# One core, one decoder layer: the high parts of the weights moved by 128 bytes in SBUF

## The chip, the cores and the metric

The kernel runs on one core of one Trainium2 chip. The metric is the time of one execution in device microseconds (us); lower is better. Times before: 1966.2 us, the median of three runs (1963.88 to 1972.04).

## The reference

One layer on 256 tokens of width 2048, all in float32: a feed-forward block, a token mixer (eight attention heads with a forget gate, four mLSTM heads) and a second feed-forward block, each with a modulated layer norm ahead and a residual layer norm behind. The weights are far larger than the activations: the two feed-forward blocks alone multiply 256 rows with 2048x11264 and 5632x2048 matrices.

```python
def _swiglu(h, w_in, w_out):
    gate, up = jnp.split(h @ w_in, 2, axis=-1)
    return (jax.nn.silu(gate) * up) @ w_out
...
    h = _swiglu(_modulate(x, sh1, sc1), ffn1_w_in, ffn1_w_out)
    x = _layernorm(ALPHA * x + 0.5 * (1 + g1) * h, ln1_g, ln1_b)
    h = _token_mixer(_modulate(x, sh2, sc2), w_in, ...)
    x = _layernorm(ALPHA * x + (1 + g2) * h, ln2_g, ln2_b)
    h = _swiglu(_modulate(x, sh3, sc3), ffn2_w_in, ffn2_w_out)
    x = _layernorm(ALPHA * x + 0.5 * (1 + g3) * h, ln3_g, ln3_b)
```

## The kernel before

**Three products for one.** Each float32 operand is split in two parts of the type that TensorE multiplies fast (`F32R`): `hi` is the value rounded to that type (a cast on ScalarE, L142), `lo` is what is left (a subtraction on VectorE, L143). `mm3` (L372 to L375) then forms one product as hi·hi, hi·lo and lo·hi, three matmuls into one accumulator. In the profile's names, `s<-xhi_f,hi_s` streams `xhi_f` through the array (the moving operand) past `hi_s`, which has been loaded into it before (the stationary operand); the row PEld LDWEIGHTS with the same names is that load.

**Two forms of product.** In form A (`cols_form_a`, L378) the weights are stationary and the activations stream, 256 columns a matmul: `s`, `gu_f`, `fh`, `fs` (input halves of the feed-forward blocks) and `pr_m`, `pr_f` (queries and keys). In form B (`out_proj`, `cols_form_b`, `cols_1024`) the rows of activations are stationary and the weights stream, up to 512 columns a matmul: `o_f` and `o_mx` (the three output projections), `mo`, `ge`, `gf`, `b_fv`, `b_mv`. In `out_proj` the stationary rows are `hh` and `hl` (feed-forward) or `yhi`, `ylo`, `yh`, `yl` (mixer).

**Where the weights go.** `load_w` (L361) reads a block of 1 MB into a buffer `raw` (three of them) and splits it into four pairs `hi`, `lo`; each of the tags `hi` and `lo` has six buffers of 4096 bytes in each partition. The pool `wp` (L52 to L61) lays out these buffers in the order in which it meets them first: the three `raw`, a filler `gap_hi`, the six `hi`, four `sums` (40 bytes each, at every 64th byte, 256 together), four `nm` (128 bytes together), the six `lo`. The functions that ask for a tile of these tags later get one of those places. All buffers of a tag stand 4096 bytes apart, and slices of them begin at multiples of 512 bytes, so that a tag has one place modulo 512 bytes. That remainder, read from the addresses in the built program, is called the place here:

| tiles | place before |
|---|---|
| `raw` (three buffers) | 96, 224, 352 |
| `hi` | 288 |
| `lo` | 160 |
| `hh`, `hl`, `yhi`, `ylo` (rows of the output projections) | 160 |
| `h` (the first pair of row tiles of each feed-forward block's output projection, made ahead) | 448 |
| `yh`, `yl` (rows of the mixer's mLSTM half) | 128 to 392, several |
| `xhi_f`, `xlo_f`, `xhi_mx`, `xlo_mx` (activations of the other products) | 480 |
| `ahi`, `alo` (parts of the modulation's sums) and, stationary beside them, `trir` | 160, 160 and 128 |

**Order.** The order of the matmuls is that of the program; a scheduling layer places the instructions of the other engines. SyncE issues the weights' DMAs, one block ahead of a free `raw` buffer. The modulation matrix (`w_ada`) is read and summed on VectorE beside the products, piece by piece, from `pump`.

Of the kernel before, what the change touches and what calls it, by code (L numbers as in the profile page):

```python
# [34 lines left out]
def layer_kernel(  # L35
# [11 lines left out]
    wp = ctx.enter_context(tc.tile_pool(name="wp", bufs=1))  # L47


    def gap(pool, nbytes, name):  # L50
        pool.tile([P, nbytes // 4], F32, tag=name, name=name)
# [1 line left out]


    wp.tile([P, 4, 520], F32, tag="raw", bufs=3, name="raw_place")
    gap(wp, 320, "gap_hi")
    wp.tile([P, 1024], F32R, tag="hi", bufs=6, name="hi_place")
    wp.tile([P, 10], F32, tag="sums", bufs=4, name="sums_place")
    wp.tile([P, 2, 3], F32, tag="nm", bufs=4, name="nm_place")
    wp.tile([P, 1024], F32R, tag="lo", bufs=6, name="lo_place")  # L60
# [1277 lines left out]
```

## Time and profile before

| | us |
|---|---|
| median of three runs | 1966.2 |
| the profiled execution | 1965.57 |
| its span, first to last instruction | 1963.8 |
| mean granted TensorE clock | 0.993 |
| first feed-forward block, input half | 33 to 541 |
| its output projection | 541 to 786 |
| mixer with its output projection | 786 to 1212 |
| second feed-forward block, input half | 1212 to 1714 |
| its output projection | 1714 to 1951 |

The profile is of one execution. Its span and what lies around it (1.8 us) make that execution's own time, which is 0.6 us under the median. A TensorE row's duration runs from the start of streaming to the modelled end of its results, and the next matmul starts long before that end; the time that a matmul takes from the path is therefore the distance from its start to the next one's start, called the spacing here. The timeline view has the starts, to 0.01 us.

### The profile page before, as it was taken

Reading aid. Unit: us, or ns where it says so; the run is one execution under the profiler, and the core shown is the slowest. Engines: PE = TensorE matmul, PEld = TensorE weight load, DVE = VectorE, ACT = ScalarE, POOL = GpSimd, SP = SyncE. Lnnn points to the kernel's source line nnn. Section 1 sums busy time; section 2 is a strip of 40 time slices with the busy share of each in tenths; the row PEclk is TensorE's granted clock in tenths of the full one; section 3 lists DMA queues with packets and bytes.
Section 4 is the critical chain, followed back from the end, with each engine's and each line's share of the span. In section 5 each row is a group of like instructions: output and inputs, shape, how many; then the busy total and the mean of one; then the engine's idle time right before and its main releaser. Section 6 shows DMA issues by size and latency. Waiting matters only on the chain.

```text
span 1963.8 us, 32259 instructions
## 1 busy us (share of the span) xinstructions
PE 1896.5 (97%) x13057; PEld 1727.6 (88%) x13057; DVE 1495.8 (76%) x1878; ACT 961.1 (49%) x1396; POOL 6.3 (0%) x17
## 2 busy tenths in 40 slices
PE   3999999999999999899999998999999999999997
PEld 3999999999988888588999786899999999988885
DVE  7788889777788897678888688777766655555776
ACT  3644354443454554745755544555444444444553
POOL 0000000000000000000000000000000000000000
PEclk9999999999999999999999999999999999999999
DMA  9998978899898786489888784888777765655552
GB/s 331 342 315 278 314 253 289 290 305 326 281 343 303 268 303 208 140 292 319 270 300 278 273 285 151 285 292 274 241 248 249 261 216 190 236 193 193 193 193 86
DMA packets 301820, 510.89 MB, mean 260 GB/s; under 512 B 10818, under 2 KB 158690, under 8 KB 300648
## 3 DMA queue, kind: packets, MB, share of 16 engines
q1 hardware_dynamic: 300808, 505.70, 76.2%
q0 software_dynamic: 864, 3.15, 0.5%
q8 instruction: 102, 1.67, 0.4%
q14 instruction: 46, 0.38, 0.0%
HBM read 506.71 MB, written 2.10 MB: 259 GB/s over the span
## 4 chain that ended last, share of the span: by engine, by line
PE 83%; DVE 8%; DMA 5%; ACT 2%; issue 2%; SPq 0%; DVEq 0%; ACTq 0%
PE gu_f L374 8%; PE gu_f L375 8%; PE gu_f L373 8%; PE o_f L373 8%; PE o_f L375 8%; PE o_f L374 8%; PE s L373 3%; PE s L375 3%; PE s L374 3%; DMA raw_s<-in_ffn_w_in_dram 2%; DVE lo_s L143 2%; PE fs L375 1%; PE fs L374 1%; PE fs L373 1%; PE o_mx L373 1%
## 5 line engine op out<-in xcount | busy, mean ns | idle before, releaser
L157 DVE SCALAR_TENSOR_TENSOR acc<-ar,csil,acc 128x1024 f32<-128x1024 f32 x242 | 307.8, 1272 | 74.6 <-DMA ar<-in_w_ada_dram 72.9
L373 PE MATMUL s<-xhi_f,hi_s 128*128 128x256 f32 x768 | 215.0, 280 | 3.0 <-ACT hi_s L142 3.0
L375 PE MATMUL s<-xhi_f,lo_s 128*128 128x256 f32 x768 | 214.4, 280 | 1.9 <-DVE lo_s L143 1.9
L374 PE MATMUL s<-xlo_f,hi_s 128*128 128x256 f32 x768 | 214.2, 279 | 0.0
L375 PE MATMUL gu_f<-xhi_f,lo_f2i 128*128 128x256 f32 x768 | 212.0, 276 | 0.0
L373 PE MATMUL gu_f<-xhi_f,hi_f2i 128*128 128x256 f32 x768 | 212.0, 276 | 0.0
L374 PE MATMUL gu_f<-xlo_f,hi_f2i 128*128 128x256 f32 x768 | 212.0, 276 | 0.0
L143 DVE TENSOR_TENSOR lo_f2i<-raw_f2i,hi_f2i 128x1024 fp32r<-128x1024 f32 x96 | 117.6, 1225 | 91.4 <-ACT hi_f2i L142 91.4
L373 PE MATMUL gu_f<-xhi_f,hi_f1i 128*128 128x256 f32 x640 | 176.8, 276 | 0.0
L375 PE MATMUL gu_f<-xhi_f,lo_f1i 128*128 128x256 f32 x640 | 176.7, 276 | 0.0
L374 PE MATMUL gu_f<-xlo_f,hi_f1i 128*128 128x256 f32 x640 | 176.7, 276 | 0.0
L142 ACT CAST hi_f2i<-raw_f2i 128x1024 fp32r<-128x1024 f32 x96 | 100.8, 1050 | 135.4 <-PE gu_f L374 124.6
L373 PEld LDWEIGHTS s<-xhi_f,hi_s 128*128 128x128 f32 x768 | 146.2, 190 | 3.5 <-ACT hi_s L142 3.4
L142 ACT CAST hi_s<-raw_s 128x1024 fp32r<-128x1024 f32 x96 | 96.6, 1049 | 107.0 <-DMA raw_s<-in_ffn_w_in_dram 85.9
L375 PEld LDWEIGHTS s<-xhi_f,lo_s 128*128 128x128 f32 x768 | 145.9, 190 | 2.9 <-DVE lo_s L143 2.8
L374 PEld LDWEIGHTS s<-xlo_f,hi_s 128*128 128x128 f32 x768 | 146.4, 191 | 0.0
L374 PEld LDWEIGHTS gu_f<-xlo_f,hi_f2i 128*128 128x128 f32 x768 | 144.2, 188 | 0.2
L373 PEld LDWEIGHTS gu_f<-xhi_f,hi_f2i 128*128 128x128 f32 x768 | 144.2, 188 | 0.2
L375 PEld LDWEIGHTS gu_f<-xhi_f,lo_f2i 128*128 128x128 f32 x768 | 144.2, 188 | 0.0
L142 ACT CAST hh<-hT 128x512 fp32r<-128x512 f32 x130 | 80.0, 622 | 127.9 <-PE o_f L374 126.6
L143 DVE TENSOR_TENSOR lo_f2o<-raw_f2o,hi_f2o 128x1024 fp32r<-128x1024 f32 x88 | 107.7, 1224 | 44.9 <-ACT hi_f2o L142 44.8
L143 DVE TENSOR_TENSOR lo_s<-raw_s,hi_s 128x1024 fp32r<-128x1024 f32 x96 | 114.5, 1221 | 30.6 <-ACT hi_s L142 30.6
(452 smaller groups left out, 5385.2 us busy)
## 6 DMA issues: line engine op xcount, KB each, us to landing
ar<-in_w_ada_dram SPq DMA_DIRECT2D x288, 512.0 KB, 5.4
raw_s<-in_ffn_w_in_dram SPq DMA_DIRECT2D x48, 1024.0 KB, 6.1
raw_f2i<-in_ffn_w_in_dram SPq DMA_DIRECT2D x48, 1024.0 KB, 5.2
raw_f1o<-in_ffn_w_out_dram SPq DMA_DIRECT2D x44, 1024.0 KB, 7.4
raw_f2o<-in_ffn_w_out_dram SPq DMA_DIRECT2D x44, 1024.0 KB, 5.1
raw_f1i<-in_ffn_w_in_dram SPq DMA_DIRECT2D x40, 1024.0 KB, 7.7
raw_mxo<-in_w_out_dram SPq DMA_DIRECT2D x16, 1024.0 KB, 6.1
raw_fh<-in_ffn_w_in_dram SPq DMA_DIRECT2D x16, 1024.0 KB, 7.3
```

Of the source, the lines that this page charges most:

```text
L142: S.copy(hi, src)
L143: return V.tensor_tensor(out=lo, in0=src, in1=hi.bitcast(F32), op=ALU.subtract)
L157: V.scalar_tensor_tensor(out=acc, in0=raw, scalar=csil[:, k:k + 1], in1=acc, op0=ALU.mult, op1=ALU.add)
L373: PE.matmul(o, ah, bh, start=start, stop=False)
L374: PE.matmul(o, ah, bl, start=False, stop=False)
L375: PE.matmul(o, al, bh, start=False, stop=stop)
```

## The change

The filler ahead of the `hi` buffers shrinks from 320 to 192 bytes, and a new filler of 128 bytes behind them keeps everything that follows where it was. The `hi` buffers move down by 128 bytes, from place 288 to place 160. No other tile moves, and the instructions of all engines, their order, their waits and the DMAs are the same, apart from the addresses of `hi`.

```diff
     wp.tile([P, 4, 520], F32, tag="raw", bufs=3, name="raw_place")
-    gap(wp, 320, "gap_hi")
+    gap(wp, 192, "gap_hi")
     wp.tile([P, 1024], F32R, tag="hi", bufs=6, name="hi_place")
+    gap(wp, 128, "gap_lo")
     wp.tile([P, 10], F32, tag="sums", bufs=4, name="sums_place")
     wp.tile([P, 2, 3], F32, tag="nm", bufs=4, name="nm_place")
     wp.tile([P, 1024], F32R, tag="lo", bufs=6, name="lo_place")
```

## The prediction

> **What bounds the kernel now.** First the page: its span, the busy shares and the chain that ended last.
>
> ```profile
> span 1963.8 us, 32259 instructions
> PE 1896.5 (97%) x13057; PEld 1727.6 (88%) x13057; DVE 1495.8 (76%) x1878; ACT 961.1 (49%) x1396; POOL 6.3 (0%) x17
> PE 83%; DVE 8%; DMA 5%; ACT 2%; issue 2%; SPq 0%; DVEq 0%; ACTq 0%
> ```
>
> TensorE sets the end: 83% of the chain is matmuls. Then the windows, to see where nothing but TensorE counts (columns: length, busy time and instructions of each engine, granted clock, DMA share and GB/s).
>
> ```profile
> core 0: us, PE busy (x) PEld busy (x) DVE busy (x) ACT busy (x) POOL busy (x), PEclk, DMA share, GB/s
> 340.00:540.00 200.00, 200.00 (x1753) 199.48 (x1752) 152.53 (x154) 85.96 (x99) 0.00 (x0) 1.00 0.92 301
> 720.00:780.00 60.00, 60.00 (x264) 49.09 (x263) 50.71 (x61) 30.19 (x39) 0.00 (x0) 1.00 0.72 244
> 1880.00:1940.00 60.00, 60.00 (x264) 49.17 (x263) 43.50 (x48) 32.34 (x42) 0.00 (x0) 1.00 0.44 149
> ```
>
> TensorE is busy throughout, at full clock. In the output projections 264 matmuls touch 60 us in both blocks, though VectorE and the DMAs are much less busy in the second: there the matmuls' own spacing is the limit. So the question is whether the spacing depends on where the operands stand. The timeline gives it (starts in the first column):
>
> ```profile
> 399.81 0.28 PE L375 MATMUL gu_f<-xhi_f,lo_f1i 128*128 128x256 f32 x1
> ...
> 400.49 0.28 PE L375 MATMUL gu_f<-xhi_f,lo_f1i 128*128 128x256 f32 x1
> 541.27 0.40 PE L373 MATMUL o_f<-hi_f1o,h 128*128 128x512 f32 x1
> ...
> 546.63 0.39 PE L375 MATMUL o_f<-hi_f1o,h 128*128 128x512 f32 x1
> 886.35 0.28 PE L373 MATMUL b_mv<-hi_mv,xhi_mx 128*128 128x256 f32 x1
> ...
> 886.70 0.28 PE L373 MATMUL b_mv<-hi_mv,xhi_mx 128*128 128x264 f32 x1
> 1900.11 0.39 PE L373 MATMUL o_f<-hi_f2o,hh 128*128 128x512 f32 x1
> ...
> 1908.81 0.39 PE L375 MATMUL o_f<-hi_f2o,hl 128*128 128x512 f32 x1
> ```
>
> Form A: 0.68 us for 6 steps, 113 ns for 256 columns. Form B in the second projection: 8.70 us for 38 steps, 229 ns for 512 columns. The same form with the rows `h` at place 448 instead of 160: 5.36 us for 23 steps, 233 ns. And 256 columns in form B: 0.35 us for 3 steps, 117 ns. The place is one thing in which the second and third differ, so it can be worth 4 ns a matmul.
>
> **Which pairs of places meet.** A stationary operand is loaded one matmul ahead (first and last start below: 546.6 against 546.9), so while one matmul streams, the next one's rows are loaded. The tile view has minimum, median and maximum durations:
>
> ```profile
> L373 PEld LDWEIGHTS o_f<-hi_f1o,hh x344: 187/188/188, 546.6 to 785.2; 128*128 128x128 f32 x172
> L373 PE MATMUL o_f<-hi_f1o,hh x344: 390/393/393, 546.9 to 785.4; 128*128 128x512 f32 x172
> L374 PE MATMUL o_f<-lo_f1o,hh x344: 388/388/397, 547.1 to 785.6; 128*128 128x512 f32 x172
> L375 PE MATMUL o_f<-hi_f1o,hl x344: 388/391/396, 547.3 to 785.9; 128*128 128x512 f32 x172
> L373 PE MATMUL o_f<-hi_f1o,h x8: 394/396/397, 541.3 to 546.2; 128*128 128x512 f32 x8
> L374 PE MATMUL o_f<-lo_f1o,h x8: 388/395/397, 541.5 to 546.4; 128*128 128x512 f32 x8
> L375 PE MATMUL o_f<-hi_f1o,h x8: 392/397/397, 541.7 to 546.6; 128*128 128x512 f32 x8
> ```
>
> In a trio of `o_f`, L373 streams `hi` (288) while rows at 160 are loaded, L374 streams `lo` (160) while rows at 160 are loaded, L375 streams `hi` (288) over rows at 160: distances of 128, 0 and 128 bytes, durations of 393, 388 and 391. After the change all three distances are 0, and the streamed place no longer changes from one matmul to the next. No row of before has both; the L374 row has the distance alone.
>
> **The change, part by part.**
>
> *Form B with rows at 160.* These are the rows `hh`, `hl`, `yhi` and `ylo`: 344 matmuls on each of three lines in each block and 64 on each of three lines of `o_mx`, which is 2 x 344 + 64 = 752 trios.
>
> ```profile
> L373 PE MATMUL o_mx<-hi_mxo,yhi 128*128 128x512 f32 x64 | 26.3, 411 | 0.0
> L373 PE MATMUL o_f<-hi_f2o,hh 128*128 128x512 f32 x344 | 135.2, 393 | 0.0
> ```
>
> Differences of durations stand here for differences of spacing, since the end is modelled from the start. Lower bound: both `hi` matmuls fall to L374's 388, (393 - 388) + (391 - 388) = 8 ns a trio, 752 x 8 ns = 6.0 us gained. Upper bound: all go to the spacing of the `h` rows, 233 against 229, so 3 x 4.1 ns x 752 = 9.2 us lost. Between them: the `hi` matmuls are nearest to their own rows and to the matched one, but L374's 388 stands between two matmuls of another place, and part of it may be a start that swings late on L373 (393) and is made good on L374. Two matmuls in a row that stream from one place (160) do exist, over another stationary place (128):
>
> ```profile
> L170 PE MATMUL bc<-alo,trir x28: 390/393/503, 359.1 to 1649.0; 128*128 128x512 f32 x28
> ```
>
> The second of such a pair takes 393, no less than the alternating ones. So I leave the two `hi` matmuls at their mean of 392 and let L374 lose half of its advantage over them, 390 instead of 388: +2 ns a trio, 752 x 2 ns = +1.5 us. TensorE has no cover there, so this goes straight to the end.
>
> *Form B with rows at 480 and the mixer's `yh`, `yl`.* Here `lo` is already at the place that `hi` will have.
>
> ```profile
> L373 PE MATMUL gf<-hi_gu,xhi_f x32: 391/392/481, 1335.9 to 1357.4; 128*128 128x512 f32 x32
> L374 PE MATMUL gf<-lo_gu,xhi_f x32: 390/392/393, 1336.2 to 1357.6; 128*128 128x512 f32 x32
> L375 PE MATMUL gf<-hi_gu,xlo_f x32: 388/391/397, 1336.4 to 1357.8; 128*128 128x512 f32 x32
> L374 PE MATMUL o_mx<-lo_mxo,yh x64: 388/393/402, 1123.9 to 1202.8; 128*128 128x512 f32 x64
> ```
>
> 392, 392, 391: against 480 the two places cost the same, so nothing. The 192 matmuls of `yh`, `yl` meet many distances already and stay near 393: nothing; at 4 ns each way they are worth 0.8 us, which both ends of the range take in.
>
> *Form A, some 9200 matmuls* (counted in the program, on each of three lines: 768 of `s`, 640 and 768 of `gu_f`, 256 each of `fh` and `fs`, 12 x 32 of `pr_m` and `pr_f`). The streamed place stays 480; two of three loads move from 288 to 160, where the third, `lo`, already is.
>
> ```profile
> L373 PE MATMUL gu_f<-xhi_f,hi_f2i x768: 276/276/279, 1446.0 to 1708.8; 128*128 128x256 f32 x192
> L374 PE MATMUL gu_f<-xlo_f,hi_f2i x768: 276/276/280, 1446.1 to 1708.9; 128*128 128x256 f32 x192
> L375 PE MATMUL gu_f<-xhi_f,lo_f2i x768: 276/276/285, 1446.3 to 1709.0; 128*128 128x256 f32 x192
> ```
>
> `lo` is loaded while L374 streams, `hi` while the other two do, and all three take 276. So nothing; the rival below has the price if that is wrong.
>
> *ScalarE's cast and VectorE's subtraction.* The cast writes `hi`, the subtraction reads it and writes `lo`, from now on at the same place.
>
> ```profile
> L142 ACT CAST hi_gu<-raw_gu x20: 612/620/674, 1234.1 to 1342.2; 128x512 fp32r<-128x512 f32 x20
> L142 ACT CAST hh<-hT x130: 612/622/639, 542.6 to 1934.4; 128x512 fp32r<-128x512 f32 x130
> L143 DVE TENSOR_TENSOR lo_gu<-raw_gu,hi_gu x20: 681/684/693, 1234.8 to 1345.0; 128x512 fp32r<-128x512 f32 x20
> L143 DVE TENSOR_TENSOR hl<-hT,hh x130: 673/688/693, 545.2 to 1935.1; 128x512 fp32r<-128x512 f32 x130
> ```
>
> At equal width, writing to 288 or 160 takes 620 and 622 ns, and subtracting with unequal or equal places (`hl` from `hh`, both 160) 684 and 688. That is at most 4 ns in 512 columns, 8 in 1024, hidden under the matmuls. Were all of VectorE's 8% of the chain (157 us) longer by 4/684, it would be 0.9 us. I take nothing.
>
> The sum: 1965.57 + 1.5 = 1967.1 us for an execution like the profiled one, which was 0.6 us under the median of the runs; on the median, **1967.7 us**.
>
> **The rivals.**
>
> *The matched place is the good one.* Streaming and loading at one place run at the L374 pace. For it: 388 is the lowest median of the 512-column rows shown, and the unmatched `h` rows the highest. Against it: the `bc` rows. Time: 1966.2 - 6.0 = 1960.2. If the constant streamed place helps on top of that, it could pass 0.5%, 9.8 us, which is about what runs of this kernel can tell from no change; that takes 13 ns a trio.
>
> *The matched place is the bad one* (slower). Streaming and loading start together and meet on the same place in every matmul, where now two of three are 128 bytes apart; L374's short row would then be the swing of its start alone. Place: the output projections. Price: the spacing of the `h` rows, 9.2 us, and 4.1 ns also on the 192 matmuls of `yh`, `yl` and the 432 of 512 columns with rows at 480 (120 of `mo`, 96 of `gf`, 24 of `ge`, 192 of `b_fv` and `b_mv`), 2.6 us: 1978.0. It decides from 4.3 ns a matmul on (9.8 us over 2256). Against it: L374 is at distance 0 now and is not slow.
>
> *Form A loses its floor.* The 113 ns hold with loads from 288, 288 and 160 in turn; 256 columns in form B take 117 with the same pair of places the other way round, so 113 is not given. If three loads from 160 cost that, 9200 x 3.4 ns = 31 us: 1997. Against it: three equal rows of 276.
>
> *The place does nothing* and the `h` rows are slow for another reason (they are the first of the projection): 1966.2. The Trainium skill says so for a part (TensorE: Matmul & The Clock Gate, "Step-by-step: what each phase is for"): TensorE has two read ports into SBUF, and loading the next weights takes no read bandwidth from the running matmul. By that rule no distance matters and the change is worth nothing; the `h` rows, 233 ns against 229, speak against it, though not alone. The same page's "Back-to-back issue gap" puts 512 columns at about 216 ns; the rows here are 13 ns above, and it does not say what they wait for.
>
> **How the numbers follow.** Forecast (spacing within some 3 ns a trio of now) 0.52; matched good 0.18; matched bad 0.18; form A 0.08; no effect of the place 0.04. The range leaves out form A and the far end beyond the `h` rows: from 1960.2 down by 3 for the spread of the runs to 1957, from 1978.0 up by 3 to 1981. Faster by over 0.5%: 0.11, all from the good match with a gain beyond L374's and a little spread. Slower by over 0.5%: form A's 0.08, two thirds of the bad match, 0.12, and 0.01 of spread: 0.21. The rest, 0.68, within.
>
> **What would show it.** In the profile after, the three lines of `o_f` should have one duration instead of three: near 391 if I am right, 388 or less if the match is good, 395 or more if it is bad. A window of 60 us in the second projection should count 264 matmuls again (267 or more: good; 260 or less: bad). The rows of `gu_f` should stay at 276 and their spacing at 113; anything else there is the costly rival. `gf` and `b_mv` should not move, nor the 1220 ns of VectorE's subtractions. I am wrong if the output projections' stages change by more than 3 us each, or any other by more than 1 us.

## The result and the profile after

| | before | after |
|---|---|---|
| median of four runs each, us | 1968.11 (1963.88 to 1972.04) | 1988.57 (1984.12 to 1991.18) |
| the profiled execution, us | 1965.57 | 1989.95 |
| its span, us | 1963.8 | 1988.2 |

The change makes the kernel slower: ratio 1.0099, 95% interval 1.0078 to 1.0120. Ratios here and below are of fast executions alone, and one of the profiles used, pair_160_32's (2017.19 us at a granted clock of 0.989), is of a slow one. The page of the kernel after, its span, busy times and the shares of the chain:

```profile
span 1988.2 us, 32259 instructions
PE 1923.7 (97%) x13057; PEld 1759.5 (88%) x13057; DVE 1496.9 (75%) x1878; ACT 961.6 (48%) x1396; POOL 6.3 (0%) x17
PE 87%; DVE 6%; DMA 4%; ACT 2%; issue 1%; SPq 0%; DVEq 0%; ACTq 0%
```

The number of instructions is the same, and VectorE and ScalarE work as long as before. TensorE is busy 27.2 us longer with the same 13057 matmuls (1923.7 - 1896.5), and the time in which it is idle (span less busy) falls by 2.8 us. So the whole loss is in matmuls that follow each other more slowly. The tile view says which (minimum, median and maximum duration in ns, first and last start in us):

```profile
L374 PE MATMUL gu_f<-xhi_f,hi_f2i x768: 276/279/283, 1465.3 to 1735.4; 128*128 128x256 f32 x192
L375 PE MATMUL gu_f<-xlo_f,hi_f2i x768: 276/279/284, 1465.5 to 1735.5; 128*128 128x256 f32 x192
L376 PE MATMUL gu_f<-xhi_f,lo_f2i x768: 276/280/285, 1465.6 to 1735.7; 128*128 128x256 f32 x192
L374 PE MATMUL o_f<-hi_f1o,hh x344: 387/389/398, 560.2 to 796.5; 128*128 128x512 f32 x172
L375 PE MATMUL o_f<-lo_f1o,hh x344: 387/389/395, 560.4 to 796.7; 128*128 128x512 f32 x172
L376 PE MATMUL o_f<-hi_f1o,hl x344: 388/389/397, 560.6 to 796.9; 128*128 128x512 f32 x172
```

Form A has left its 276: `gu_f` of the second block now runs from 1465.3 to 1735.7, 270.4 us where it was 263.0 (1446.0 to 1709.0). Form B in the output projections has become shorter: the three durations 393, 388 and 391 are one, 389, and the first projection takes 236.7 us from its first `hh` to its last `hl`, where it was 239.0. From the first and last starts of such rows, in both kernels:

| stretch, us | before | after | difference |
|---|---|---|---|
| `s` and `gu_f`, first block | 37.8 to 541.2 | 37.7 to 554.4 | +13.3 |
| `o_f`, `hh` and `hl`, first block | 546.9 to 785.9 | 560.2 to 796.9 | -2.3 |
| from there to the first `fh` (mixer, boundary, `ge`) | 785.9 to 1242.4 | 796.9 to 1255.2 | +1.8 |
| `fh` | 1242.4 to 1335.0 | 1255.2 to 1350.6 | +2.8 |
| `gf`, to the first `fs` | 1335.0 to 1358.1 | 1350.6 to 1374.0 | +0.3 |
| `fs` and `gu_f`, second block | 1358.1 to 1709.0 | 1374.0 to 1735.7 | +10.8 |
| from there to the last `o_f` | 1709.0 to 1950.7 | 1735.7 to 1975.1 | -2.3 |

With what lies between the rows they make the span's 24.4. Summed over starts: 9110 spacings of form A without a wait grow from a mean of 113.52 to 117.00 ns (+31.7 us), and 2110 of `o_f` shrink from 229.07 to 226.94 (-4.5 us); together that is the 27.2 us of busy time.

The mean of 117.0 is not one pace but two. Windows of 40 us of after in form A and one of 60 us in the second projection (TensorE's columns come first; the counts include the two or three matmuls that only reach into a window):

```profile
400.00:440.00 40.00, 40.00 (x342) 40.00 (x342) 29.86 (x29) 16.21 (x18) 0.00 (x0) 1.00 0.97 320
465.00:505.00 40.00, 40.00 (x356) 40.00 (x355) 31.31 (x31) 15.82 (x19) 0.00 (x0) 1.00 0.97 325
1560.00:1600.00 40.00, 40.00 (x342) 40.00 (x341) 23.07 (x22) 15.49 (x17) 0.00 (x0) 1.00 0.74 252
1880.00:1940.00 60.00, 60.00 (x267) 49.69 (x266) 45.57 (x51) 34.57 (x45) 0.00 (x0) 1.00 0.57 193
```

342 or 356 of the same matmuls fit into 40 us: 117.7 or 113 ns each. The first two windows, one of each pace, have the same clock (1.00) and the same DMA share (0.97), and nearly as much work on VectorE and ScalarE beside them; the third is slow at a DMA share of 0.74. In the kernel before, the first two of these windows hold 353 and 355. Where the pace changes, the timeline of after shows it (starts in the first column):

```profile
458.82 0.28 PE L375 MATMUL gu_f<-xlo_f,hi_f1i 128*128 128x256 f32 x1
458.94 0.28 PE L376 MATMUL gu_f<-xhi_f,lo_f1i 128*128 128x256 f32 x1
459.05 0.28 PE L374 MATMUL gu_f<-xhi_f,hi_f1i 128*128 128x256 f32 x1
459.17 0.28 PE L375 MATMUL gu_f<-xlo_f,hi_f1i 128*128 128x256 f32 x1
459.29 0.28 PE L376 MATMUL gu_f<-xhi_f,lo_f1i 128*128 128x256 f32 x1
459.41 0.39 PE L171 MATMUL bc<-ahi,trir 128*128 128x512 f32 x1
459.63 0.39 PE L171 MATMUL bc<-alo,trir 128*128 128x512 f32 x1
459.87 0.28 PE L374 MATMUL gu_f<-xhi_f,hi_f1i 128*128 128x256 f32 x1
459.98 0.28 PE L375 MATMUL gu_f<-xlo_f,hi_f1i 128*128 128x256 f32 x1
...
461.11 0.28 PE L376 MATMUL gu_f<-xhi_f,lo_f1i 128*128 128x256 f32 x1
461.23 0.28 PE L374 MATMUL gu_f<-xhi_f,hi_f1i 128*128 128x256 f32 x1
```

Four steps take 0.47 us ahead of the two `bc` matmuls (458.82 to 459.29) and twelve take 1.36 us behind them (459.87 to 461.23): 117.5 and 113 ns. TensorE does nothing else between. At 519.7 us two more `bc` matmuls turn the pace back. In groups of six matmuls of form A with no wait in them, 1211 of 1478 are slow in after (a mean spacing above 115.5 ns); in before it is 33 of 1479, all within a dozen matmuls behind an interruption. So before, form A falls back to 113 ns each time; after, it keeps whichever pace an interruption leaves it in.

### The profile page after: what moved, and what is told of

Same layout as the page of the kernel before. It is cut to its first block, busy times and chain, and to the rows that moved or that the text cites. A ratio compares the mean times of both kernels' runs of the same rounds, so it can differ in the third digit from the quotient of the medians.

```text
span 1988.2 us, 32259 instructions
## 1 busy us (share of the span) xinstructions
PE 1923.7 (97%) x13057; PEld 1759.5 (88%) x13057; DVE 1496.9 (75%) x1878; ACT 961.6 (48%) x1396; POOL 6.3 (0%) x17
## 4 chain that ended last, share of the span: by engine, by line
PE 87%; DVE 6%; DMA 4%; ACT 2%; issue 1%; SPq 0%; DVEq 0%; ACTq 0%
PE gu_f L376 8%; PE gu_f L374 8%; PE gu_f L375 8%; PE o_f L374 8%; PE o_f L375 8%; PE o_f L376 8%; PE s L376 3%; PE s L374 3%; PE s L375 3%; DMA ar<-in_w_ada_dram 2%; PE pr_f L374 2%; PE fs L374 2%; PE pr_f L376 2%; PE fs L376 2%; PE pr_f L375 2%; PE fs L375 2%
## 5 line engine op out<-in xcount | busy, mean ns | idle before, releaser
L374 PE MATMUL s<-xhi_f,hi_s 128*128 128x256 f32 x768 | 217.0, 283 | 4.8 <-ACT hi_s L143 3.0
L374 PE MATMUL gu_f<-xhi_f,hi_f2i 128*128 128x256 f32 x768 | 213.8, 278 | 0.0
L144 DVE TENSOR_TENSOR lo_f2i<-raw_f2i,hi_f2i 128x1024 fp32r<-128x1024 f32 x96 | 117.5, 1224 | 98.2 <-ACT hi_f2i L143 98.1
L374 PE MATMUL gu_f<-xhi_f,hi_f1i 128*128 128x256 f32 x640 | 178.3, 279 | 0.1
L374 PEld LDWEIGHTS s<-xhi_f,hi_s 128*128 128x128 f32 x768 | 145.9, 190 | 5.6 <-ACT hi_s L143 3.3
L374 PEld LDWEIGHTS gu_f<-xhi_f,hi_f2i 128*128 128x128 f32 x768 | 143.9, 187 | 0.2
L144 DVE TENSOR_TENSOR lo_f2o<-raw_f2o,hi_f2o 128x1024 fp32r<-128x1024 f32 x88 | 107.7, 1224 | 44.3 <-ACT hi_f2o L143 44.2
```

Source lines behind the costliest of these rows:

```text
L144: return V.tensor_tensor(out=lo, in0=src, in1=hi.bitcast(F32), op=ALU.subtract)
L374: PE.matmul(o, ah, bh, start=start, stop=False)
```

## The experiments

Places are given modulo 512 bytes in the text and the diffs, and modulo 256 in the tables, since the runs show that only that counts. "Distance" is the streamed place less the place of the operand loaded meanwhile, modulo 256. In form A the high part is loaded while the first and third line of `mm3` stream, the low part while the second does; in before the distances are 192, 64, 192, in after 64, 64, 64.

**Which part is it: both at 288, exchanged, both at 480, x split.** Each kernel moves places and nothing else; the instructions and their order are those of before. (Beside the parts of the weights, small tiles such as `nm` and `sums` move in some of these kernels and in those of the next two sections, and the layer norms' `n`, `sq` and `xf` in those that move x. No product of form A or B reads them.) The first three edits are against the kernel before, the last against the kernel after:

```diff
 # both_288: hi and lo at 288
-    gap(wp, 320, "gap_hi")
+    wp.tile([P, 2, 3], F32, tag="nm", bufs=4, name="nm_place")
+    gap(wp, 192, "gap_1")
     wp.tile([P, 1024], F32R, tag="hi", bufs=6, name="hi_place")
+    wp.tile([P, 1024], F32R, tag="lo", bufs=6, name="lo_place")
     wp.tile([P, 10], F32, tag="sums", bufs=4, name="sums_place")
-    wp.tile([P, 2, 3], F32, tag="nm", bufs=4, name="nm_place")
-    wp.tile([P, 1024], F32R, tag="lo", bufs=6, name="lo_place")
+    gap(wp, 128, "gap_5")
 # swapped ("exchanged" in the text): hi at 160, lo at 288
-    gap(wp, 320, "gap_hi")
+    wp.tile([P, 2, 3], F32, tag="nm", bufs=4, name="nm_place")
+    gap(wp, 64, "gap_1")
     wp.tile([P, 1024], F32R, tag="hi", bufs=6, name="hi_place")
+    gap(wp, 128, "gap_3")
+    wp.tile([P, 1024], F32R, tag="lo", bufs=6, name="lo_place")
     wp.tile([P, 10], F32, tag="sums", bufs=4, name="sums_place")
-    wp.tile([P, 2, 3], F32, tag="nm", bufs=4, name="nm_place")
-    wp.tile([P, 1024], F32R, tag="lo", bufs=6, name="lo_place")
+    gap(wp, 128, "gap_6")
 # both_480: hi and lo at 480, as x
-    gap(wp, 320, "gap_hi")
     wp.tile([P, 1024], F32R, tag="hi", bufs=6, name="hi_place")
+    wp.tile([P, 1024], F32R, tag="lo", bufs=6, name="lo_place")
     wp.tile([P, 10], F32, tag="sums", bufs=4, name="sums_place")
     wp.tile([P, 2, 3], F32, tag="nm", bufs=4, name="nm_place")
-    wp.tile([P, 1024], F32R, tag="lo", bufs=6, name="lo_place")
+    gap(wp, 320, "gap_4")
 # x_split: as after, xhi of the feed-forward blocks at 352, xlo at 480
-        return (xp.tile([P, KD, T], F32R, name=f"xhi_{tag}"), xp.tile([P, KD, T], F32R, name=f"xlo_{tag}"))
+        xhi = xp.tile([P, KD, T], F32R, name=f"xhi_{tag}")
+        if tag != "mx":
+            gap(xp, 128, f"gap_{tag}")
+        return xhi, xp.tile([P, KD, T], F32R, name=f"xlo_{tag}")
```

> hi and lo both at place 288, nothing else moved. Theory 1 (variety: form A falls back to its 113 ns only where the loads come from two places in turn): all loads come from one place, so the 256-column matmuls stand at 117 to 118 ns for most of their time as in the changed kernel, near 1990 us. Theory 2 (the place itself: loads from 160 are the slow ones over streams at 480, loads from 288 are good): 113 ns throughout, near 1968 us. In form B with rows at 160 both give a distance of 128 for all three, about 229 ns.

> hi at 160 and lo at 288, nothing else moved. Theory 1: two places in turn again, 113 ns in form A, and the output projections between 227 and 231 ns: within 6 us of the kernel before, near 1968 us. Theory 2: two of three loads still come from 160, 116 to 118 ns, near 1985 us.

> hi and lo both at place 480, the same as the streamed activations of form A. Theory 1: one place, so 117 to 118 ns for most of form A, 1985 to 1995 us. Theory 2 says nothing certain of this place; 113 ns here would speak against theory 1. Form B with rows at 160 has a distance of 320 for all three.

> The changed kernel (hi and lo at 160) with xhi of the two feed-forward blocks moved to 352 and xlo left at 480, so that the streamed place alternates in form A and the loads' does not. Theory 1 in its wide form (any alternation of the distance brings the 113 ns back): 113 ns in the feed-forward blocks, the output projections keep the 227 ns of the changed kernel, so 3 to 6 us under the kernel before, near 1964 us. Theory 1 in its narrow form (the loads' places must alternate) and theory 2: 116 to 118 ns, near 1985 us.

All four are slow: ratios to the kernel before 1.0133 (1.0109 to 1.0156), 1.0081 (1.0056 to 1.0105), 1.0268 (1.0250 to 1.0285) and 1.0108 (1.0093 to 1.0123). So neither of the first two theories holds: by the first, exchanged was to be fast, by the second, both_288. x_split refutes the first in its wide form too. The tile view of both_480:

```profile
L373 PE MATMUL gu_f<-xhi_f,hi_f2i x768: 277/283/283, 1481.6 to 1759.5; 128*128 128x256 f32 x192
L373 PE MATMUL o_f<-hi_f1o,hh x344: 396/397/398, 564.8 to 807.7; 128*128 128x512 f32 x172
L373 PE MATMUL gf<-hi_gu,xhi_f x32: 387/389/482, 1366.7 to 1387.9; 128*128 128x512 f32 x32
L374 PE MATMUL gf<-lo_gu,xhi_f x32: 389/389/397, 1367.0 to 1388.2; 128*128 128x512 f32 x32
L375 PE MATMUL gf<-hi_gu,xlo_f x32: 389/389/397, 1367.3 to 1388.4; 128*128 128x512 f32 x32
```

With x and weights at one place form A is at its worst, 283 (a spacing of 120 ns, 336 matmuls in 40 us; no theory had more than 118), while in form B `gf`, whose rows stand at 480 too, is now the fast one (389, spacing 227) and `o_f`, whose rows stand at 160, is slow (397, spacing 233). One place for all is bad in form A and good in form B.

The first line of what follows is from both_288, the other three are from x_split:

```profile
L374 PE MATMUL o_f<-hi_f1o,hh x344: 390/393/404, 558.4 to 801.1; 128*128 128x512 f32 x172
L377 PE MATMUL gu_f<-xhi_f,hi_f2i x768: 278/281/283, 1463.7 to 1736.6; 128*128 128x256 f32 x192
L378 PE MATMUL gu_f<-xlo_f,hi_f2i x768: 279/282/283, 1463.8 to 1736.7; 128*128 128x256 f32 x192
L379 PE MATMUL gu_f<-xhi_f,lo_f2i x768: 277/280/283, 1464.0 to 1736.8; 128*128 128x256 f32 x192
```

In both_288 all three lines of form B's `o_f` stream from one place, 128 bytes from the rows; they take 393 each at the median, no better than the unmatched ones before. So a constant streamed place alone is not the gain. In x_split the lines of `gu_f` have medians of 281, 282 and 280 and each of the three windows of form A counts 342: never fast, with the distances of before (192, 64, 192). What differs from before is that the streamed place changes from one matmul to the next and the loaded one does not.

**The period.** The three pairs 160/32, 288/32 and 224/160 (high, low), the first two of which differ from exchanged and from both_288 by 256 bytes in the low part alone; and the kernel before with the high part 256 bytes lower. All four edits are against the kernel before:

```diff
 # pair_160_32
-    gap(wp, 320, "gap_hi")
+    gap(wp, 192, "gap_0")
     wp.tile([P, 1024], F32R, tag="hi", bufs=6, name="hi_place")
     wp.tile([P, 10], F32, tag="sums", bufs=4, name="sums_place")
     wp.tile([P, 2, 3], F32, tag="nm", bufs=4, name="nm_place")
     wp.tile([P, 1024], F32R, tag="lo", bufs=6, name="lo_place")
+    gap(wp, 128, "gap_5")
 # pair_288_32
-    gap(wp, 320, "gap_hi")
+    wp.tile([P, 2, 3], F32, tag="nm", bufs=4, name="nm_place")
+    gap(wp, 192, "gap_1")
     wp.tile([P, 1024], F32R, tag="hi", bufs=6, name="hi_place")
     wp.tile([P, 10], F32, tag="sums", bufs=4, name="sums_place")
-    wp.tile([P, 2, 3], F32, tag="nm", bufs=4, name="nm_place")
     wp.tile([P, 1024], F32R, tag="lo", bufs=6, name="lo_place")
+    gap(wp, 128, "gap_5")
 # pair_224_160
-    gap(wp, 320, "gap_hi")
+    wp.tile([P, 10], F32, tag="sums", bufs=4, name="sums_place")
     wp.tile([P, 1024], F32R, tag="hi", bufs=6, name="hi_place")
-    wp.tile([P, 10], F32, tag="sums", bufs=4, name="sums_place")
     wp.tile([P, 2, 3], F32, tag="nm", bufs=4, name="nm_place")
+    gap(wp, 320, "gap_3")
     wp.tile([P, 1024], F32R, tag="lo", bufs=6, name="lo_place")
 # mod256: hi at 32, lo at 160
-    gap(wp, 320, "gap_hi")
+    gap(wp, 64, "gap_0")
     wp.tile([P, 1024], F32R, tag="hi", bufs=6, name="hi_place")
-    wp.tile([P, 10], F32, tag="sums", bufs=4, name="sums_place")
     wp.tile([P, 2, 3], F32, tag="nm", bufs=4, name="nm_place")
     wp.tile([P, 1024], F32R, tag="lo", bufs=6, name="lo_place")
+    wp.tile([P, 10], F32, tag="sums", bufs=4, name="sums_place")
+    gap(wp, 256, "gap_5")
```

> hi at 160 as in the changed kernel, lo at 32, 128 bytes below hi as in the kernel before; nothing else moved. Theory 3 (form A falls back to 113 ns when lo stands 128 bytes below hi, wherever the two stand): 113 ns in form A throughout, the three lines of the output projections between 227 and 232 ns, 1960 to 1975 us against some 1970 of the kernel before. Theory 2 (loads from 160 are slow in themselves) or chance: 116 to 118 ns, 1985 us or more.

> hi at 288 as in the kernel before, lo at 32, 256 bytes below it. Theory 3 with exactly 128: stretches at 117 to 118 ns in form A, 1985 us or more. Theory 3 with any lo below hi: 113 ns. In the profile: the mean spacing of gu_f.

> lo at 160 as in both kernels, hi at 224, 64 bytes above it: half of the distance that the change took away. Theory 3 with exactly 128: stretches at 117 ns or more; with any lo below hi: 113 ns. Form B may be slower where the distance to the rows is no multiple of 128 bytes: hi streams at 64 from them.

> The kernel before with the high parts of weights moved by 256 bytes, to 32, low parts still at 160. Theory (places count modulo 256): as before in every spacing, gu_f 113.4, o_f sum 687: 1966 to 1972, ratio 0.998 to 1.002. Rival (modulo 512, as the change's words have it): gu_f leaves 113 and the time rises by over 10 us.

Pair 160/32 has the medians of the exchanged pair line for line (278, 281, 278 in `gu_f`; 395, 394, 393 in the first `o_f`), at ratio 1.0110 (1.0079 to 1.0141). 288/32 was executed once, in 1990.83 us. In the second block it has the medians of both_288 (281 three times in `gu_f`, 393 in `o_f`); in the first it does not: `gu_f` was mostly fast (276), and `o_f` has 394, 395 and 394. So the two agree in part alone, and one execution cannot say whether that is more than the change of pace that form A shows anyway. 224/160 was executed once too, in 2000.16 us, with 283, 283 and 278. The theory that the low parts must stand 128 bytes below the high ones, from which 160/32 was to be fast, falls. The last kernel gives the period for the high parts; its rows are those of before, `gu_f` and `o_f`:

```profile
L374 PE MATMUL gu_f<-xhi_f,hi_f2i x768: 276/276/279, 1452.1 to 1714.8; 128*128 128x256 f32 x192
L374 PE MATMUL o_f<-hi_f1o,hh x344: 390/393/393, 550.2 to 788.8; 128*128 128x512 f32 x172
L375 PE MATMUL o_f<-lo_f1o,hh x344: 388/388/397, 550.4 to 789.0; 128*128 128x512 f32 x172
L376 PE MATMUL o_f<-hi_f1o,hl x344: 388/391/396, 550.7 to 789.2; 128*128 128x512 f32 x172
```

Ratio 0.9994 (0.9978 to 1.0010). With the medians of 160/32 this says that places count modulo 256 bytes: the change moved the high parts by half a period.

**Does a place count by itself, or only the distance?** The exchanged pair again, with x of the two feed-forward blocks moved along, to 352; all three operands of form A there stand 128 bytes lower than in before. The mixer's x stays at 480.

```diff
 # all_down: swapped, and in new_xT
...
+        if tag != "mx":
+            gap(xp, 128, f"gap_{tag}")
+        return xhi, xlo
```

> The pair 160 for high and 288 for low parts, which was slow in form A with x at 480 (gu_f 117.2/120.6/117.6, time 1988.5), now with x of the two feed-forward blocks at 352: all three operands of form A there lie 128 bytes below those of the kernel before. Theory R (only distances modulo 256 count): s, gu_f, fh and fs at 113.4 again, the mixer's pr_* slow still: about 1968 to 1976. Theory A (each place by itself): gu_f 117 or more, about 1985 to 1995.

```profile
L379 PE MATMUL gu_f<-xhi_f,hi_f2i x768: 276/276/284, 1452.3 to 1715.1; 128*128 128x256 f32 x192
L380 PE MATMUL gu_f<-xlo_f,hi_f2i x768: 276/276/281, 1452.4 to 1715.2; 128*128 128x256 f32 x192
L381 PE MATMUL gu_f<-xhi_f,lo_f2i x768: 276/276/283, 1452.5 to 1715.3; 128*128 128x256 f32 x192
L380 PE MATMUL pr_f<-xlo_mx,hi_f2a x32: 277/281/285, 974.0 to 986.8; 128*128 128x256 f32 x32
```

The feed-forward rows are back at 276, where the same weights at the same places had 278, 281 and 278 beside x at 480; the mixer's `pr_f`, with x left behind, is slow (281). Ratio 1.0016 (0.9999 to 1.0032), against the exchanged pair's 1.0081. So no place is bad by itself; the arrangement is.

| mod 256: x; hi, lo | distances in form A | `gu_f` medians, second block |
|---|---|---|
| 224; 32, 160 (before, mod256) | 192, 64, 192 | 276, 276, 276 |
| 96; 160, 32 (all_down) | 192, 64, 192 | 276, 276, 276 |
| 224; 160, 160 (after) | 64, 64, 64 | 279, 279, 280 (two paces) |
| 224; 32, 32 (both_288) | 192, 192, 192 | 281, 281, 281 (two paces in the first block) |
| 224; 160, 32 (exchanged) | 64, 192, 64 | 278, 281, 278 (some fast) |
| 224; 224, 160 | 0, 64, 0 | 283, 283, 278 |
| 224; 224, 224 (both_480) | 0, 0, 0 | 283, 283, 283 |
| 96 and 224; 160, 160 (x_split) | 192, 64, 192 | 281, 282, 280 |

**What helps form B.** The kernel before with the rows moved instead of the weights: `hh` and `yhi` at 288, `hl` and `ylo` at 160, so that every distance in the projections is 0 while the streamed place still alternates.

```diff
-    for t in ("hhi", "hlo"):
-        lnp.tile([P, 2, T], F32R, tag=t, bufs=6, name=f"{t}_place")
+    lnp.tile([P, 2, T], F32R, tag="hlo", bufs=6, name="hlo_place")
+    gap(lnp, 128, "gap_hh")
+    lnp.tile([P, 2, T], F32R, tag="hhi", bufs=6, name="hhi_place")
...
-    yhi, ylo = (lnp.tile([P, NFH, T], F32R, name=f"y{i}") for i in ("hi", "lo"))
+    ylo = lnp.tile([P, NFH, T], F32R, name="ylo")
+    gap(lnp, 128, "gap_yhi")
+    yhi = lnp.tile([P, NFH, T], F32R, name="yhi")
```

> The kernel before (hi 288, lo 160) with the rows of the output projections moved instead: hh and yhi to 288, hl and ylo left at 160, so that hi streams over loads of hh at 288 and lo over loads of hl at 160. Form A is untouched: 113 ns. Theory B1 (the 227 ns of the changed kernel come from streaming and loading at one place): 227 ns on all three lines, 2 ns on 2256 matmuls, 4 to 5 us faster than the kernel before. Theory B2 (they come from a streamed place that does not change): about 229 ns as before, no change.

```profile
L373 PE MATMUL o_f<-hi_f1o,hh x344: 387/388/398, 552.5 to 793.0; 128*128 128x512 f32 x172
L374 PE MATMUL o_f<-lo_f1o,hh x344: 392/395/399, 552.7 to 793.2; 128*128 128x512 f32 x172
L375 PE MATMUL o_f<-hi_f1o,hl x344: 387/390/395, 553.0 to 793.5; 128*128 128x512 f32 x172
```

Slower: 241.0 us (552.5 to 793.5) for the stretch that took 239.0 in before and 236.7 in after; ratio 1.0024 (1.0005 to 1.0043). Match alone does nothing good, and neither does a constant place alone (both_288). Both together give 227 ns, in `o_f` of after and in `gf` of both_480.

**The two parts, one at a time.** If form A alone loses and form B alone gains, a kernel whose form A reads the high parts at before's place and whose form B reads them at after's must beat both. The first version keeps the six buffers one behind the other in one tile:

```diff
-    wp.tile([P, 1024], F32R, tag="hi", bufs=6, name="hi_place")
-    gap(wp, 128, "gap_lo")
+    his = wp.tile([P, 6 * 1024 + 32], F32R, tag="his", name="his")
+    nhi = [0]
+    def hi_tile(n, form_a):
+        o = nhi[0] % 6 * 1024 + 32 * form_a    # places_turned: not form_a
+        nhi[0] += 1
+        return his[:, o:o + n]
...
```

The lines not shown let `load_w` and the blocks of `gf` ask `hi_tile` for their buffers.

> The changed kernel with the high parts at two places: in form A (s, gu_f, fh, fs, pr_*) at 288, as in the kernel before, in form B (o_f, o_mx, mo, ge, gf, b_*) at 160, as in the changed kernel; the buffers lie one behind the other in one tile with 128 bytes over, the order of the instructions is as before but for the first rows of the first output projection. Theory (the loss is form A's alone, and what decides there is the pair of places of the weights against x; form B gains from matched and constant places): gu_f spacing 113.4 ns, o_f 227, so the time before less about 752 trios x 6.5 ns = 5 us: 1962 to 1968, ratio 0.9975. Rival (the step between buffers, or the transitions between the forms, set the slow pace): gu_f stays at 116 to 117 and the time near 1988. Rival (the gain of form B is paid back elsewhere, since what waits there is not TensorE): ratio 0.999 to 1.001 with o_f at 227.

> The same kernel with the two places exchanged: form A reads the high parts at 160 (as in the changed kernel), form B at 288 (as in the kernel before). Theory: the whole loss of form A without the gain of form B: gu_f 116 to 118, o_f 232/226/228 (687 ns for three), so the changed kernel's time plus about 5 us: 1990 to 1996. Rival (the loss sits in what lies around form B): at most 1975.

The spacings came out as the theory has them: 113.5 and 227.0 ns in two_places, 116.9 and 229.1 in places_turned. The times did not: ratios 1.0029 (1.0011 to 1.0047) and 1.0142 (1.0126 to 1.0158). In two_places TensorE waits (waits view in three windows: engine, tile and line waited for, us in total, times, longest):

```profile
PE o_f L380 <- ACT his L149: 1.7, 2, 1.1
PE o_f L381 <- DVE lo_f1o L150: 0.5, 1, 0.5
...
PE gf L380 <- ACT his L149: 3.6, 1, 3.6
...
PE o_f L380 <- ACT his L149: 1.1, 1, 1.1
```

These 6.9 us stand at the three changes from form A to form B and shortly behind one of them. There the first buffer at the new offset shares 128 bytes with the last one at the old, so that its cast can start only when that one has been read. That this makes the waits is argued and not shown by itself: in these two kernels the scheduling layer also put many instructions of ScalarE, VectorE and the DMAs into another order than that of before, far beyond the first rows of the first output projection. The cast that `gf` waits for, for example, starts at 1339.61 us, behind four casts of `xhi_f`. So these two times hold more than places. The second version takes six separate buffers of 4224 bytes, which leaves every instruction in the order of before (`...` stands for lines not shown):

```diff
-    gap(wp, 320, "gap_hi")
-    wp.tile([P, 1024], F32R, tag="hi", bufs=6, name="hi_place")
+    wp.tile([P, 1], F32, tag="rq1", bufs=2, name="rq1_place")
+    wp.tile([P, 2, 3], F32, tag="nm", bufs=4, name="nm_place")
+    for i in range(6):
+        wp.tile([P, 1056], F32R, tag=f"hi{i}", name=f"hi_place{i}")
...
+    def hi_tile(n, name, form_a):
+        i = nhi[0] % 6
+        nhi[0] += 1
+        o = 32 * (i % 2 != form_a)    # places_turned_6tiles: ==
+        return wp.tile([P, 1056], F32R, tag=f"hi{i}", name=name)[:, o:o + n]
...
```

Each buffer begins 128 bytes further, modulo 256, than the one ahead of it, so the offset `o` alternates as well. To make room, a small tile (`rq1`) moves into this pool and three fillers of other pools shrink. By that the rows `hh`, `hl`, `yhi` and `ylo` come to stand at 416, which is 160 modulo 256 as before, and `h` at 384; x stays. The two versions share all of this.

> The two places again (form A reads high parts at 32 modulo 256, form B at 160), now in six buffers that do not touch, each 128 bytes longer than before, so that every instruction stands in the order of the kernel before and no buffer of one form overlaps one of the other. Theory (form A's pace is the whole loss, form B's matched and constant place a gain of 4 to 6 us, and the 7 us of waits in the run with one tile came from the overlap at the changes of form): gu_f 113.4 ns, o_f 227, ratio to the kernel before 0.996 to 0.9985. Rival (the waits are not from the overlap, or form B's gain is lost in later waits): ratio 0.9995 or more with the same spacings.

> The same six buffers with the two places exchanged (form A 160, form B 32 modulo 256). Theory: form A's loss alone, without form B's gain and without the overlap's waits: the changed kernel's time plus 4 to 6 us, ratio to the kernel before 1.012 to 1.0145, gu_f 116 to 118, o_f 687 ns for three. Rival (the loss hangs on the whole layout, not on form A's pair of places): ratio within 0.003 of 1.

> The changed kernel once more beside the two above, on the same chip. Theory (one part form A's loss, one part form B's gain): its ratio lies below that of the turned places by 0.002 to 0.003, and above that of the two places by 0.012 to 0.015. Rival: the three do not add up.

| kernel | form A, form B read hi at (mod 256) | median, us | ratio to before | form A / `o_f` spacing, ns |
|---|---|---|---|---|
| two_places_6tiles | 32, 160 | 1962.31 (9 runs) | 0.9972 (0.9960 to 0.9984) | 113.5 / 226.9 |
| before | 32, 32 | 1967.74 (14 runs) | 1 | 113.5 / 229.1 (its profile) |
| changed_again | 160, 160 | 1984.04 (4 runs) | 1.0087 (1.0068 to 1.0106) | 116.7 / 226.9 |
| places_turned_6tiles | 160, 32 | 1989.61 (4 runs) | 1.0111 (1.0093 to 1.0128) | 117.0 / 229.0 |

The tile view of two_places_6tiles, its form A and its form B:

```profile
L382 PE MATMUL gu_f<-xhi_f,hi_f2i x768: 276/276/279, 1447.5 to 1710.2; 128*128 128x256 f32 x192
L382 PE MATMUL o_f<-hi_f1o,hh x344: 389/389/398, 546.8 to 783.1; 128*128 128x512 f32 x172
L383 PE MATMUL o_f<-lo_f1o,hh x344: 387/389/389, 547.1 to 783.3; 128*128 128x512 f32 x172
L384 PE MATMUL o_f<-hi_f1o,hl x344: 388/389/396, 547.3 to 783.6; 128*128 128x512 f32 x172
```

And of places_turned_6tiles:

```profile
L382 PE MATMUL gu_f<-xhi_f,hi_f2i x768: 276/280/283, 1458.2 to 1730.6; 128*128 128x256 f32 x192
L382 PE MATMUL o_f<-hi_f1o,hh x344: 390/393/393, 555.6 to 794.1; 128*128 128x512 f32 x172
```

two_places_6tiles has form A as before, form B as after, and is faster than both kernels: by 0.28% than before, by 1.14% than the changed one (0.9972 / 1.0087). The parts add up. Form A alone costs 0.0111, form B alone gains 0.0028, which makes 0.0083 where the changed kernel shows 0.0087, well within the intervals. In us, from the medians: 21.9 lost and 5.4 gained, 16.4 beside a measured 16.3. The waits of two_places are gone too: in the same windows around the three changes the waits view of two_places_6tiles is empty for TensorE. The turned kernel fell just short of the ratio expected of it (1.012), and the distance from the two places to the changed kernel is 0.0115 where 0.012 to 0.015 was expected; the distance from the turned to the changed kernel, 0.0024, is as expected (0.002 to 0.003).

## Why the prediction was wrong

**The step that failed** is "Form A, some 9200 matmuls": "`lo` is loaded while L374 streams, `hi` while the other two do, and all three take 276. So nothing". It took each load by itself: if `lo` costs nothing at 160 beside a stream at 480, three loads from 160 should not. The runs show that a load has no price of its own. The low part at 160 is free beside a high part 128 bytes off and not free beside one at 160; all_down makes the slow pair 160/32 fast by moving x alone. Three equal rows of 276 were evidence for the arrangement of before as a whole and for nothing else. The rival "Form A loses its floor" had the size right, 113 to 117 and 31 us (measured: 113.5 to 117.0 in the mean, 31.7 us), as "the costly rival", with a chance of 0.08. That the size fits so well is in part luck: its 117 came from `b_mv` in form B, while the measured 117.0 is a mean of two paces, 113 and 117.7, which nothing in the prediction foresaw, and at another common place (both_480) it is 120. Its 1997 lies above the 1988.57 measured for two reasons: form B's gain, and waits that shrink when TensorE is slower. In places_turned_6tiles, which has no gain of form B, 9128 spacings without a wait are 3.47 ns longer than in before, 31.7 us, and the span grows by 21.9 (1985.7 - 1963.8); what makes up for the rest is that fewer spacings have a wait in them and these take less (TensorE's idle time falls by 5.6 us). The page of after shows the same in small (idle time down by 2.8 us). The time is above the range, which left form A out.

**Form B with rows at 160** was taken at +1.5 us, between -6.0 and +9.2; it is -4.5 us in the spacings of `o_f` and -5.4 us in the time. The rival "the matched place is the good one" had the sign and nearly the size (-6.0), but not the reason: matched_rows has the match and is slower. The hi rows fell from 393 and 391 to 389, and the matched row did not keep its 388 but rose to 389. That fits the reading that L374's 388 was partly the swing of a late neighbour; but the neighbours fell by more than it rose, so the sign taken was wrong. The `bc` rows, which spoke against, have a constant place without a match (160 over 128), and both_288 shows that this is not enough.

**Form B with rows at 480** was put at nothing, since the two places cost the same there. It moved, and not only in `gf`, which has 394 on all three lines where it had 392, 392 and 391:

```profile
L374 PE MATMUL gf<-hi_gu,xhi_f x32: 394/394/483, 1351.5 to 1373.3; 128*128 128x512 f32 x32
```

The mean spacing of `gf` went from 230.3 to 233.4 ns, that of `mo` from 228.7 to 231.6, and that of the 512 columns of `b_mv` from 230.6 to 233.2: some 3 ns on the 432 matmuls of 512 columns with rows at 480, 1.3 us, a constant streamed place without a match again. (The 1.8 us by which the mixer's stretch grew hold this in part, and also 1152 matmuls of `pr_m` and `pr_f`, form A, nearly all at the slow pace; shorter waits take some of both back.)

**ScalarE and VectorE** are as forecast: busy 961.6 and 1496.9 us, against 961.1 and 1495.8; the subtraction of `lo_f2i` takes 1224 ns, where it took 1225.

**"The place does nothing"** is refuted. The rule named there, that loading the next weights takes no read bandwidth from the running matmul (Trainium skill, TensorE: Matmul & The Clock Gate, "Step-by-step: what each phase is for"), does not fit these runs: two_places_6tiles and places_turned_6tiles issue the same instructions in the same order and differ in where form A's stationary high part and form B's streamed one stand, and form A is at 113.5 in one and 117.0 in the other. No run shows what the two reads meet on.

**What would show it** worked: "The rows of `gu_f` should stay at 276 and their spacing at 113; anything else there is the costly rival" is the line that decided. The window of the second projection counts 267 matmuls, the mark set for a good match.

## What to carry to other kernels

Where TensorE is the bound, an address is a parameter of its spacing: look at the starts of consecutive matmuls (here 113 or 117 ns for 256 columns, 227 to 233 for 512) before trusting that two layouts are equal, and judge a layout by streamed and loaded operands together, not operand by operand. Two forms of product may want the same tile at different places; giving each its own cost 128 bytes a buffer here and was worth more than either common place. A median that lies between two values in the tile view (279 with a minimum of 276) may be two paces, and windows that count matmuls separate them.

## What the hardware showed that was not expected

- The spacing of these matmuls depends on addresses modulo 256 bytes: 256 bytes off changed nothing (mod256: 0.9994, the same medians on every line quoted), 128 bytes off cost 4 ns in 256 columns, and streaming and loading at the same place in form A cost 6.5 (113.5 to 120.0).
- One arrangement can have two paces, 113 and 117.7 ns, and hold either for hundreds of matmuls until other matmuls or a wait interrupt it. Which one follows an interruption repeats in part: in both executions of the changed kernel that were profiled, form A has the same long stretches from 380 us to the end of the first block (in groups of six: slow 112, fast 88, slow 48) and from some 1510 us to the end of the second (fast 16, slow 216, fast 88); between 1274 and 1318 us the second execution is fast where the first is slow. What chooses the pace is open. In the changed kernel a weight load starts 3.4 ns behind the stream beside it in the fast pace and 2.5 ns in the slow one (means over after), but in x_split, slow throughout, it is 3.3 ns, so that is not what sets it.
- The distance between streamed and loaded operand is not the whole rule: x_split has the distances of before and is slow throughout, and in form B the match pays only with a constant streamed place (227 ns; 231 with match alone in matched_rows, 229 and 233 with constancy alone in `gf` and `o_f` of both_288). Nor does the distance decide in form B: `gf` of both_288 and `o_f` of both_480 both stream from one place, 64 from the rows, and take 229.0 and 233.4 ns. In form A no arrangement that stayed at 113 ns streams from two places, but only x_split had two; more was not tried.
